# Priority offsets of the delta-rule recurrence against the projections scheduled beside it

## The chip, the cores and the metric

The kernel runs on one core of one Trainium2 chip. The metric is the device time of one execution, in microseconds; lower is better. The core has five engines that run side by side: TensorE (PE, matmuls), VectorE (DVE), ScalarE (ACT), GpSimd (POOL) and SyncE (SP, which issues most DMAs). Each engine takes its instructions in the order in which the compiled program lists them, and waits where an operand is not there yet.

## The reference

One inference step of a hybrid decoder layer over a prompt of 2048 tokens and 8 x 8 sample tokens, width 1024. RMSNorm and one input projection feed three groups of heads: A, an RWKV-7 mixer with a matrix state; B, an RG-LRU; C, an S5 state space model. Their outputs go through one output projection, then a SwiGLU block, a gated embedding and a last norm. The part that matters here is A's recurrence, which runs token by token in the reference:

```python
def step(s, inp):
    r_t, w_t, k_t, v_t, kk_t, a_t = inp
    s_kk = jnp.einsum('bhij,bhj->bhi', s, kk_t)
    s = (s * w_t[:, :, None, :]
         - s_kk[..., None] * (kk_t * a_t)[:, :, None, :]
         + v_t[..., None] * k_t[:, :, None, :])
    return s, jnp.einsum('bhij,bhj->bhi', s, r_t)
```

Its output gets a group norm per head, a bonus and a gate. The mixed rows of A, B and C, 512 + 256 + 256, are multiplied by `w_out`.

## The kernel before

The program has three stages. `phase1a` (to about 640 us) does the norm and the input projection. The sequence stage, `Phase1b.run` with `Mixers` (about 640 to 1462 us), does the recurrence, the mixers of B and C, and the output projection. `phase2` (the rest) does the SwiGLU block, the embedding and the last norm, in three blocks of 704 tokens; its first matmul is L2164.

In the sequence stage the recurrence is cut into 32 chunks of 64 tokens, in 8 units of 4 chunks. Eight heads lie in four pairs, so one product of a chunk is eight matmuls on tiles of 64 x 64 or 128 x 64 of the array, in f32. `chunk(j)` (L1607) holds the chain from state to state. In the rows its parts are: `ps_r` (L1623), the state times the chunk's keys; `R` (L1624), its copy on ScalarE; `ps_u` (L1602), the solve with the inverted triangle `Xg`; `UV` (L1605), two copies on ScalarE; `ps_s` (L1638), the update; and `SV` (L1641), two sums on VectorE that make the next state. `ps_yt` (L1650) is the chunk's output, copied to `ysb` (L1653) and stored to `yy`. Beside the chain, `front` and `prepare` make the scores of the next chunk (`ps_ak` L1533, `ps_rb` L1539, masked on VectorE) and its scaled keys (`ps_bk` L1559, `BKt` L1560), `merge` joins the inverted 32 x 32 blocks of the next unit (`ps_y` L1418, `ps_x` L1427), and `load_chunk` and `load_v` load AR, BK, UV and SV. SV and UV have two buffers each, AR three.

The other work of the stage is: the mixers of B and C (`Mixers`, among others L1099, L1189, L1263, L1264, L1284, L186); `groups_bc`, the output projection of B's and C's rows, a unit of 256 tokens at a time, each 96 matmuls of 128 x 256 with the operand `mb` (helper `mm3`, L59 to L61, in fp32r); `groups_a`, the same for A's rows with the operand `ma`, each after a group norm of its unit (`ps_cm` and `ps_var` L1819, square L1839, done in two halves, with two PSUM buffers between them); and the sample step (`sample`, `sample_a`). `groups_a` and the sample step come when `groups_bc` is done, since they reuse its memory.

What sets the order: the generators of these parts are stepped in turns (`turns`, L1958), and this gives each instruction its place in program order. A scheduler then orders each engine's instructions by simulating the program: of those that are ready it takes the one with the highest priority, which is the place in program order, moved ahead by the offset of a `high_priority` block. Four offsets stand in the recurrence: CHAIN for the links from state to state, FRONT for scores, keys, merges and loads, and OUT for the output. Mixers and projections have none. In short form, from `chunk`:

```python
            with self.tc.high_priority(offset=FRONT):
                self.front(j + 1)
                self.prepare(j + 1)
...
        with self.tc.high_priority(offset=CHAIN):
            self.solve(self.psk, X, R, UV, "ps_u")
        yield
...
        with self.tc.high_priority(offset=OUT):
            ps = self.psf("ps_yt")
```

Of the kernel before, what the change touches and what calls it, by code (L numbers as in the profile page):

```python
# [1313 lines left out]
GN_EPS = 64e-5  # L1314
NU = SEQ // 256
HALF = (slice(0, 64), slice(64, 128))
CHAIN = 300
STEP0 = 0
FRONT = 200
OUT = 200  # L1320
SMP0 = 4
SMPO = 4
MIX = 3.0
# [9 lines left out]
def halves(x):  # L1333

    return x[0:64, :, 0], x[64:128, :, 1]


class Phase1b:
# [144 lines left out]
    def chain(self):  # L1483

        yield from self.early()
        for u in range(NU):
# [4 lines left out]
            for j in range(4):  # L1491
                for _ in self.chunk(u * 4 + j, lambda h, c: self.Xg[u][h, 4 * j + c]):
                    slot += 1
                    if slot in MERGE:
                        with self.tc.high_priority(offset=FRONT):
                            next(mg, None)
                    yield
            with self.tc.high_priority(offset=FRONT):
                for _ in mg:
# [107 lines left out]
    def chunk(self, j, X):  # L1607
# [3 lines left out]
        if j < 4 * NU - 1:  # L1611
# [3 lines that stand above are left out]
        t0 = self.s2.tile([P, 4, 64], F32, name="t0")  # L1615
        R = self.s2.tile([P, 4, 64], F32, name="R")
        with self.tc.high_priority(offset=CHAIN):
            for h, x in zip(HALF, halves(SV)):
# [6 lines left out]
# [3 lines that stand above are left out]
# [3 lines left out]
        if j < 4 * NU - 1:  # L1631
            with self.tc.high_priority(offset=FRONT):
                self.load_v(SVn, j + 1)
        with self.tc.high_priority(offset=CHAIN):
            ps = self.psk("ps_s")
# [6 lines left out]

        with self.tc.high_priority(offset=OUT):
            ps = self.psf("ps_yt")
# [11 lines left out]
        if j < 4 * NU - 2:  # L1656
            with self.tc.high_priority(offset=FRONT):
                self.load_chunk(j + 2)
# [860 lines left out]
```

## Time and profile before

| | us |
|---|---|
| time, median of 3 runs | 3219.71 (3216.01 to 3224.82) |
| profiled execution, its own time | 3217.54 |
| its span, first to last instruction | 3215.8 |
| TensorE busy | 3022.9 |
| VectorE busy | 2134.8 |
| ScalarE busy | 1407.5 |
| GpSimd busy | 648.7 |

Times of instructions come from one profiled execution. A start is measured; the end of a matmul is modelled, so the distance from one start to the next says more than a matmul's own duration. An f32 matmul leaves two records, an fp32r matmul (the projections) one. The granted clock (PEclk) is the share of TensorE's full rate that the chip grants: 1.00 is 2.4 GHz, 0.50 is 1.2 GHz, and what lies between is a mean of the two.

### The profile page before, as it was taken

How to read it: one execution, taken by the hardware profiler on the slowest of the kernel's cores; microseconds unless marked ns; L12 is line 12 of the kernel's file. 1: busy time of each engine (PE TensorE's matmuls, PEld its weight loads, DVE VectorE, ACT ScalarE, POOL GpSimd, SP SyncE). 2: the span in 40 equal slices, each digit the busy share in tenths (PEclk: the TensorE clock that was granted, in tenths of full speed). 3: DMA queues.
4: the chain of work that ended last, by engine and by line, in shares of the span. 5: the costliest groups of instructions: out<-in, count | busy, mean ns of one | idle time of the engine just before them, and what ended most of it. 6: DMA issues, size and time to landing. Idle time of an engine off the chain costs nothing. (4 is left out here: it accounts for less than half of the span.)

```text
span 3215.8 us, 55092 instructions
## 1 busy us (share of the span) xinstructions
PE 3022.9 (94%) x21490; PEld 2740.7 (85%) x21490; DVE 2134.8 (66%) x3819; ACT 1407.5 (44%) x2566; POOL 648.7 (20%) x783
## 2 busy tenths in 40 slices
PE   8999999868899999996999998999999899999988
PEld 6798777656777787775999998999999899999988
DVE  4866758978764244258666676876667587667676
ACT  6555654436553333144333335533333553333354
POOL 1324434434443342230000003200000230000010
PEclk9999999958996898797999999999999999999999
DMA  6564765596654574272222223242222324222223
GB/s 198 150 186 127 212 182 158 160 234 166 175 165 134 153 211 123 70 203 94 73 75 76 72 74 103 79 133 73 73 79 70 104 72 136 79 73 79 71 78 113
DMA packets 597709, 392.92 MB, mean 122 GB/s; under 512 B 176316, under 2 KB 555720, under 8 KB 597448
## 3 DMA queue, kind: packets, MB, share of 16 engines
q1 hardware_dynamic: 589720, 371.43, 39.8%
q0 software_dynamic: 4880, 17.57, 1.5%
q8 instruction: 169, 2.77, 0.4%
q14 instruction: 92, 0.75, 0.1%
q10 hardware_dynamic: 2848, 0.40, 0.1%
HBM read 292.69 MB, written 96.62 MB: 121 GB/s over the span
## 5 line engine op out<-in xcount | busy, mean ns | idle before, releaser
L54 ACT CAST w<-raw 128x512 fp32r<-128x512 f32 (+1 forms) x438 | 258.1, 592 | 449.4 <-PE po L2141 115.2
L55 DVE TENSOR_TENSOR w<-raw,w 128x512 fp32r<-128x512 f32 (+1 forms) x438 | 303.1, 694 | 166.7 <-ACT w L54 151.9
L2151 POOL TENSOR_TENSOR acc<-acc,sq 128x704 f32<-128x704 f32 x35 | 61.7, 1762 | 1401.7 <-ACT sq L2150 1399.5
L2140 PE MATMUL po<-u,w 128*128 128x352 f32 x1056 | 341.1, 323 | 0.0
L2141 PE MATMUL po<-u,w 128*128 128x352 f32 x1056 | 340.3, 323 | 0.0
L2139 PE MATMUL po<-u,w 128*128 128x352 f32 x1056 | 324.1, 324 | 5.8 <-ACT u L54 5.8
L61 PE MATMUL ps_d<-xk,wlo 128*128 128x512 f32 (+1 forms) x800 | 286.6, 358 | 9.3 <-DVE wlo L55 9.3
L59 PE MATMUL ps_d<-xk,whi 128*128 128x512 f32 (+1 forms) x800 | 284.9, 358 | 8.1 <-ACT q__5803 L761 3.9
L54 ACT CAST w<-s 128x512 fp32r<-128x512 f32 x264 | 163.5, 621 | 290.1 <-PE po L2141 128.1
L60 PE MATMUL ps_d<-xk,whi 128*128 128x512 f32 (+1 forms) x800 | 286.0, 358 | 2.2 <-DVE xk L314 2.2
L2140 PE MATMUL pB<-xc,w 128*128 128x352 f32 x792 | 257.6, 325 | 5.6 <-DVE xc L55 5.6
L2139 PE MATMUL pB<-xc,w 128*128 128x352 f32 x792 | 256.9, 324 | 0.8 <-ACT xc L54 0.8
L2141 PE MATMUL pB<-xc,w 128*128 128x352 f32 x792 | 255.8, 323 | 0.0
L2309 DVE TENSOR_TENSOR h<-h,po 128x352 f32<-128x352 f32 x288 | 141.5, 517 | 109.5 <-PE po L2141 109.3
L55 DVE TENSOR_TENSOR w<-s,w 128x512 fp32r<-128x512 f32 x264 | 182.5, 692 | 46.7 <-ACT w L54 42.4
L2139 PEld LDWEIGHTS po<-u,w 128*128 128x128 f32 x1056 | 195.3, 188 | 6.6 <-ACT u L54 6.4
L2140 PEld LDWEIGHTS po<-u,w 128*128 128x128 f32 x1056 | 199.2, 189 | 0.9 <-DVE u L55 0.9
L2141 PEld LDWEIGHTS po<-u,w 128*128 128x128 f32 x1056 | 199.2, 189 | 0.0
L2139 PE MATMUL pA<-xc,w 128*128 128x352 f32 x528 | 173.7, 329 | 8.0 <-ACT p L2265 4.9
L61 PEld LDWEIGHTS ps_d<-xk,wlo 128*128 128x128 f32 x800 | 152.0, 190 | 31.8 <-DVE wlo L55 12.0
L2140 PE MATMUL pA<-xc,w 128*128 128x352 f32 x528 | 173.2, 328 | 5.3 <-DVE xc L55 5.3
L59 PEld LDWEIGHTS ps_d<-xk,whi 128*128 128x128 f32 x800 | 151.4, 190 | 29.7 <-ACT whi L54 5.1
(1004 smaller groups left out, 8106.2 us busy)
## 6 DMA issues: line engine op xcount, KB each, us to landing
raw<-in_w_ffn_up_dram SPq DMA_DIRECT2D x132, 512.0 KB
w<-in_w_in_dram SPq DMA_DIRECT2D x80, 512.0 KB
raw<-in_w_ffn_down_dram SPq DMA_DIRECT2D x48, 512.0 KB
sc_hT<-hp POOLq DMA_DIRECT2D x32, 512.0 KB, 4.1
raw<-in_w_ple_gate_dram SPq DMA_DIRECT2D x32, 512.0 KB
mat<-sc_mats SPq DMA_DIRECT2D x24, 512.0 KB
h<-sc_hT SPq DMA_DIRECT2D x32, 352.0 KB
raw<-in_w_ffn_down_dram SPq DMA_DIRECT2D x24, 384.0 KB
```

What stands on the lines that cost most here:

```text
L54: nc.scalar.copy(hi, src)
L55: nc.vector.tensor_sub(lo, src, hi.bitcast(F32))
L59: nc.tensor.matmul(ps, whi, xhi, start=first, stop=False)
L60: nc.tensor.matmul(ps, whi, xlo, start=False, stop=False)
L61: nc.tensor.matmul(ps, wlo, xhi, start=False, stop=last)
L2139: nc.tensor.matmul(ps, whi, xhi, start=first, stop=False, skip_group_check=more)
L2140: nc.tensor.matmul(ps, whi, xlo, start=False, stop=False, skip_group_check=more)
L2141: nc.tensor.matmul(ps, wlo, xhi, start=False, stop=last, skip_group_check=more)
L2151: eng.tensor_add(acc, acc, sq)
L2309: nc.vector.tensor_add(h[d2 * 2 + dd][:, ss], h[d2 * 2 + dd][:, ss], po[:, :SUB])
```

## The change

Three of the offsets change: CHAIN from 300 to 3000, FRONT from 200 to 2900, OUT from 200 to 2800. Nothing else does: the same instructions run on the same engines.

```diff
--- before.py
+++ after.py
@@ -1314,10 +1314,10 @@
 GN_EPS = 64e-5
 NU = SEQ // 256
 HALF = (slice(0, 64), slice(64, 128))
-CHAIN = 300
+CHAIN = 3000
 STEP0 = 0
-FRONT = 200
-OUT = 200
+FRONT = 2900
+OUT = 2800
 SMP0 = 4
 SMPO = 4
 MIX = 3.0
```

The order of the compiled program shows what that moves. It is the same up to the first chunks of the recurrence, and the same again from the last projections on. On TensorE, the update of chunk 15 (counted from 0) stands so before, `ps_s` being the update and `ps_d` a projection of B's and C's rows:

```order
L61 MATMUL ps_d<-mb,w1lo 128x256
L1638 MATMUL ps_s<-UV,BKt 64x64
L59 MATMUL ps_d<-mb,w1hi 128x256
L1638 MATMUL ps_s<-UV,BKt 64x64
L60 MATMUL ps_d<-mb,w1hi 128x256
L1638 MATMUL ps_s<-UV,BKt 64x64
L61 MATMUL ps_d<-mb,w1lo 128x256
L1638 MATMUL ps_s<-UV,BKt 64x64
L59 MATMUL ps_d<-mb,w1hi 128x256
```

And so after:

```order
L1602 MATMUL ps_u<-R,Xg_6553 64x64 x8
L1533 MATMUL ps_ak<-AR,BK 64x128 x8
L1650 MATMUL ps_yt<-AR,SV 64x64 x5
L1263 MATMUL ps_y<-U,mat 128x72
L1264 MATMUL ps_y<-H,mat 128x72
L1263 MATMUL ps_y<-U,mat 128x72
L1650 MATMUL ps_yt<-LB,UV 64x64
L1264 MATMUL ps_y<-H,mat 128x72
L1638 MATMUL ps_s<-UV,BKt 64x64 x8
L1650 MATMUL ps_yt<-LB,UV 64x64 x7
L59 MATMUL ps_d<-mb,w1hi 128x256
L60 MATMUL ps_d<-mb,w1hi 128x256
L61 MATMUL ps_d<-mb,w1lo 128x256
```

Before, every matmul of the update has a projection matmul behind it; after, the eight stand together, and the output products stand together too. The same chunk's two links on ScalarE, from the copy `R` to the copies `UV`, stand so before (the rows between are mixers, table loads and a merge):

```order
L1624 COPY R<-ps_r 128x256
L180 ACTIVATE sq<-gr 128x512
L156 CAST hi<-sq 128x512
L1265 COPY x_9708<-ps_y 128x256 x2
L188 ACT_TABLE_LOAD
L188 ACTIVATE rs<-rs 128x512
L189 ACT_TABLE_LOAD
L189 ACTIVATE rs<-rs 128x512
L1430 ACTIVATE Xg_6552<-ps_x_10755 32x16x32 x2
L1605 ACTIVATE UV<-ps_u 64x4x64 x2
```

And so after:

```order
L1624 COPY R<-ps_r 128x256
L1109 ACTIVATE gr<-gr,nsp 128x512
L1560 COPY BKt<-ps_bk 128x512
L168 ACTIVATE gq<-gl 128x512
L1265 COPY x_7850<-ps_y 128x288
L1120 ACT_TABLE_LOAD
L1120 ACTIVATE gr<-gr 128x512
L1605 ACTIVATE UV<-ps_u 64x4x64 x2
```

Ten rows have become eight; mixer instructions and a table load still stand between the links. In the second half of the stage TensorE's order before goes on to mix chunks and projections, while after it has no chunk left there. A piece from where the group norm (`ps_cm`, `ps_var`), the sample step (`ps_ry`) and the projection of A's rows meet, after the change:

```order
L61 MATMUL ps_d<-ma,w0lo 128x256
L59 MATMUL ps_d<-ma,w0hi 128x256
L60 MATMUL ps_d<-ma,w0hi 128x256
L61 MATMUL ps_d<-ma,w0lo 128x256
L1728 MATMUL ps_ry<-ax,S_11725 64x2x8 x5
L1819 MATMUL ps_cm<-hl,cm 128x512 x2
L59 MATMUL ps_d<-ma,w0hi 128x256
L60 MATMUL ps_d<-ma,w0hi 128x256
L61 MATMUL ps_d<-ma,w0lo 128x256
L59 MATMUL ps_d<-ma,w0hi 128x256
```

The recurrence's last chunk is done before this place, 1218 projection matmuls ahead of the last projection; before the change 240 were left.

## Rows read from the trace of the kernel before

**Rows 1.** page, parts 1 and 2: TensorE's busy time, share, instructions; granted clock

```profile
PE 3022.9 (94%) x21490; PEld 2740.7 (85%) x21490; DVE 2134.8 (66%) x3819; ACT 1407.5 (44%) x2566; POOL 648.7 (20%) x783
...
PEclk9999999958996898797999999999999999999999
```

**Rows 2.** windows, sequence stage: stretch, length, busy us per engine, PEclk, DMA share, GB/s

```profile
640.00:740.00 100.00, 65.45 (x785) 52.40 (x785) 75.61 (x132) 34.51 (x61) 35.56 (x42) 0.61 0.81 202
740.00:795.00 55.00, 44.13 (x707) 31.41 (x708) 46.98 (x73) 38.59 (x65) 24.41 (x28) 0.93 0.67 175
...
985.00:1060.00 75.00, 73.36 (x337) 52.62 (x337) 23.99 (x47) 12.15 (x21) 13.75 (x16) 0.55 0.29 78
...
1215.00:1385.00 170.00, 167.49 (x1572) 124.31 (x1567) 58.98 (x122) 43.56 (x102) 45.57 (x60) 0.80 0.36 102
...
sum 822.00, PE 749.91 PEld 583.67 DVE 441.66 ACT 332.83 POOL 294.49; mean PE 107.13 PEld 83.38 DVE 63.09 ACT 47.55 POOL 42.07
```

**Rows 3.** timeline, TensorE: start, us, line, out<-in; turn-taking at low clock

```profile
1011.02 0.41 PE L60 MATMUL ps_d<-mb,w1hi 128*128 128x256 f32 x1
1011.23 0.41 PE L61 MATMUL ps_d<-mb,w1lo 128*128 128x256 f32 x1
...
1013.14 0.48 PE L1650 MATMUL ps_yt<-AR,SV 128*64 128x64 f32 x2
1013.54 0.58 PE L60 MATMUL ps_d<-mb,w1hi 128*128 128x256 f32 x1
1014.06 0.48 PE L1650 MATMUL ps_yt<-AR,SV 128*64 128x64 f32 x2
```

**Rows 4.** timeline, TensorE: turn-taking at full clock

```profile
1341.35 0.32 PE L1539 MATMUL ps_rb<-AR,BK 64*64 64x64 f32 x2
1341.61 0.38 PE L61 MATMUL ps_d<-ma,w0lo 128*128 128x256 f32 x1
1341.92 0.33 PE L1539 MATMUL ps_rb<-AR,BK 64*64 64x64 f32 x2
```

**Rows 5.** timeline, TensorE: projections in a row, and the stall behind them

```profile
1460.89 0.28 PE L60 MATMUL ps_d<-ma,w0hi 128*128 128x256 f32 x1
1461.01 0.28 PE L61 MATMUL ps_d<-ma,w0lo 128*128 128x256 f32 x1
1472.33 0.96 PE L2164 MATMUL ps_st<-ah,ones 128*128 128x352 f32 x2 [11.04 <-ACT ah L54]
```

**Rows 6.** timeline, TensorE: recurrence matmuls in a row at full clock

```profile
753.04 0.69 PE L1650 MATMUL ps_yt<-AR,SV 128*64 128x64 f32 x16
753.66 0.51 PE L1650 MATMUL ps_yt<-LB,UV 64*64 64x64 f32 x10
```

**Rows 7.** timeline, TensorE: two recurrence products taking turns

```profile
937.27 0.33 PE L1638 MATMUL ps_s<-UV,BKt 128*64 128x64 f32 x2
937.53 0.33 PE L1539 MATMUL ps_rb<-AR,BK 64*64 64x64 f32 x2
937.78 0.33 PE L1638 MATMUL ps_s<-UV,BKt 128*64 128x64 f32 x2
```

**Rows 8.** VectorE: timeline of two chunk sums, then the line's first and last start

```profile
746.58 0.85 DVE L1641 TENSOR_TENSOR SV<-t,ps_s 64x256 f32<-64x256 f32 x2
...
791.08 0.42 DVE L1641 TENSOR_TENSOR SV<-t,ps_s 64x256 f32<-64x256 f32 x1
...
L1641 DVE TENSOR_TENSOR SV<-t,ps_s x64: 384/419/426, 701.7 to 1419.6; 64x256 f32<-64x256 f32 x64
```

**Rows 9.** ScalarE: timeline of group norm squares, then the line's first and last start

```profile
1410.01 0.60 ACT L1839 ACTIVATE sqb<-ps_cm 128x512 f32<-128x512 f32 x1 [0.87 <-PE ps_cm L1819]
...
1418.02 0.60 ACT L1839 ACTIVATE sqb<-ps_cm 128x512 f32<-128x512 f32 x1 [0.40 <-PE ps_cm L1819]
...
L1839 ACT ACTIVATE sqb<-ps_cm x18: 278/597/602, 1128.9 to 1440.2; 128x512 f32<-128x512 f32 x16, 128x128 f32<-128x128 f32 x2
```

## Prediction

> **What bounds the kernel now.** I read the page first, then the windows over the sequence stage, then the timeline of TensorE inside it. Matmuls fill 94% of the span [rows 1], which would say that nothing but fewer matmuls helps. The granted clock says otherwise: in its 40 slices it is near full, save between the ninth and the nineteenth, where the sequence stage lies [rows 1]. The windows cut that stage out, from 640 to 1462 us [rows 2]. TensorE counts as busy there for 749.91 of 822 us, while VectorE has 441.66, ScalarE 332.83 and GpSimd 294.49 [rows 2]. So TensorE is the engine that the stage waits for; the question is what its busy time consists of. Two windows stand out: 985 to 1060 and 1215 to 1385 have TensorE 98% busy, at a clock of 0.55 and 0.80, with VectorE at about a third of the time [rows 2].
>
> The timeline shows what runs there. One small recurrence matmul and one projection matmul take turns, and a pair takes 1014.06 - 1013.14 = 0.92 us [rows 3]. Just before, projections in a row start 0.21 us apart, at the same low clock [rows 3]. At full clock the same kind of turn-taking costs 1341.92 - 1341.35 = 0.57 us a pair [rows 4]. In a row, a projection costs 0.12 us [rows 5], and recurrence matmuls cost (753.66 - 753.04) / 8 = 0.078 us each; each f32 matmul leaves two records, so x16 is eight [rows 6]. A round trip from projection to recurrence and back therefore adds 0.57 - 0.12 - 0.078 = 0.37 us to work that is the same. Two recurrence products of different tile shape that take turns show it too: 937.78 - 937.27 = 0.51 us for two matmuls, so 0.35 us added [rows 7]. What bounds the stage is how often TensorE changes between kinds, and the low clock that goes with it.
>
> **The change part by part.** Only the order of instructions moves, so every term is a number of places in the order times a price from rows. I take all matmuls from the first of the recurrence to the last of the second projection, 4756 in both orders.
>
> A. Projection and recurrence. The order before has 541 places where one stands next to the other, the order after has 61. That is 240 round trips fewer, at 0.37 us: 89 us. I take the full-clock price and count the clock apart. At the low clock a pair adds 0.92 - 0.21 - 2 x 0.078 = 0.55 us [rows 3], so the upper bound is 132 us.
>
> B. Other changes of kind. All places where the groups projection, recurrence, mixers, group norm and sample step meet fall from 1093 to 511, which is 102 beyond A, or 51 round trips at 0.37: 19 us. Inside the recurrence, places between different products fall from 337 to 240, or 48 round trips at 0.35: 17 us. Some of these may keep the tile shape and cost nothing, so the bounds are 0 and 36; I take 36, since the row that I have shows the cost.
>
> C. The clock. Time at the lower of the two levels, 1.2 GHz, is twice the lack of granted clock: 2 x 0.45 x 75 + 2 x 0.20 x 170 = 135.5 us in the two windows [rows 2]. Work there would run twice as fast at 2.4 GHz, which gives back 68 us. A has taken part of that: of a pair of 0.92 us, all that can go is 0.92 - 0.20 = 0.72, A took 0.37, so 0.35 is left where half of the pair would be 0.46. Three quarters of 68 is 51 us. Bounds 0 (the new order is as slow elsewhere) and 68.
>
> D. Cover lost. The recurrence is a chain: product, copy on ScalarE, product, copy, product, sum on VectorE. Where it runs without projections, from 740 to 795, TensorE idles 10.9 of 55 us [rows 2] in about five chunks, so 2.0 us a chunk. The order before has eight chunks ahead of the first projection, the order after twelve, and then all 20 others with only 366 of the 1584 projection matmuls between them (44 us of work). So 24 more chunks run thinly covered: 24 x 2.0 = 48 us at most, 0 at least. I take 36, near the upper end, because on ScalarE six other rows still stand between the two links of chunk 15, a table load among them.
>
> Loads: the queue of SyncE is reordered with it, chunk loads first. They were waiting at most in the start, where the DMA share is 0.81 [rows 2]; a chunk pace twice as fast raises the share of the middle from 0.67 towards that, so I count nothing for them here and leave it to the slow rival. The tail after the last projection is untouched: its order is the same in both, and the 11.04 us stall there [rows 5] stays.
>
> Sum: 89 + 36 + 51 - 36 = 140 us. The profiled execution took 3217.54 us, 1.7 us around its span; 3217.5 - 140 = 3077.5. The median of before is 2.2 us above the profiled run, so about 3080.
>
> A second way gives the same. Chunk sums without projections beside them follow each other by (791.08 - 746.58) / 4 = 11.1 us, against (1419.6 - 701.7) / 31 = 23.2 us over the whole stage [rows 8]. At 11.1 us the 29 chunks after the one at 746.58 end near 1069. Behind them stand 1218 projection matmuls (146 us at 0.12), 72 of group norm (17 us at twice that), 288 of the sample step (22 us at 0.078), some 6 us of mixers and 215 changes of kind (40 us at 0.37 a round trip): about 231 us, so the last projection starts near 1300 plus some waits, against 1461 [rows 5]. That is 130 to 160 us.
>
> **The rivals.** First, the group norm takes over. Behind the recurrence, each half group goes through ScalarE, VectorE, TensorE and back. The closest that its squares follow each other is 1418.02 - 1410.01 = 8.0 us; over the stage it is (1440.2 - 1128.9) / 17 = 18.3 us [rows 9]. Eighteen halves at 8 us are 144 us, hidden beside the roughly 185 us that TensorE still has from the first of them on (960 projections at 0.12, and the group norm, sample step and changes of kind as above); from 10.3 us on they set the pace. At 13 us they take 234 us, so 49 us of the gain go: 3130. For it speaks that the two buffers of its PSUM pool hold one half at a time; against it that its slow stretches before are those of turn-taking. Chance 0.15.
>
> Second, more than I count: A at its upper bound, C whole and D nearly nothing, 132 + 36 + 68 - 10 = 226, so about 2990. Turn-taking lies mostly in the low-clock windows, which speaks for it. Chance 0.12.
>
> Third, slower: the chain itself becomes the bound. It decides at (1461 - 231 - 747) / 29 = 16.7 us a chunk. At 20 us the recurrence ends at 1327, the last projection at about 1560, 100 us later than now: 3320. The mechanism is the queue of ScalarE and of the loads: a link that finds six mixer instructions ahead of it, or a state buffer whose load is issued only when the output product two chunks back has read it, with the DMA engines at a share of 0.8. For it: 23.2 us is the pace now. Against it: 11.1 us was reached with VectorE 85% busy [rows 2, 8], and the slow pace lies where projections take turns. The Trainium skill, Perfetto Trace Analysis, section Optimization Strategy, advises interleaving regimes that are bound by different engines; by that rule this change goes the wrong way. The rows do not bear the rule out here: where the two are interleaved finest, both run slowest [rows 3]. Chance 0.07.
>
> Fourth, the clock stays low. A recurrence with small gaps could keep TensorE at 1.2 GHz until it ends. From 640 to 740, where it starts up with gaps, the granted clock is 0.61 [rows 2]. The 322 us from 747 to 1069 hold about 80% matmul work, 258 us at a clock of 0.93; at 0.61 that is 258 x 0.93 / 0.61 = 393, so 135 us more, and nearly all is lost: about 3215. Against it: 740 to 795 holds the same mix, without projections, at 0.93 [rows 2]. The Trainium skill, TensorE: Matmul & The Clock Gate, section Part 1: The HAM clock gate, says that the low clock is the default and that activity releases it, which fits both stretches and does not choose between them. Chance 0.04.
>
> That the change does not do what it says is ruled out by the order itself: the 32nd chunk now stands ahead of 1218 projection matmuls.
>
> **How the numbers follow.** Forecast 0.60, group norm 0.15, more 0.12, slower 0.07, clock 0.04, and 0.02 for an exchange of one loss for another at no change. A difference of 0.3% (10 us) is about what a measurement of this kernel can tell. The first three are faster: 0.60 + 0.15 + 0.12 = 0.87. The clock rival and the exchange are within 0.3%, 0.06, of which I give 0.01 to the slow side, since the clock rival's own spread reaches there: 0.05 the same, 0.08 slower. The predicted time is that of the forecast, 3080. The range takes in the group norm's 3130 with its spread, up to 3150, and reaches down to 3010, about half the way to the second rival's bound with the upper price of A; it leaves out the slow and the clock rivals and the far part of the second, together under 0.2.
>
> **What would show it.** In the profile after: TensorE's clock near full between the eleventh and the seventeenth slice; no stretch where single projections and recurrence matmuls alternate; chunk sums 10 to 13 us apart and the last near 1070 (above 16.7 us apart, the third rival); the last projection near 1320; squares of the group norm 8 to 10 us apart (above, the first rival). The prediction is wrong if the price of a change of kind does not carry over, because the recurrence's wait for ScalarE sits where the round trip sat, or if the clock stays at 0.6 while the chain runs alone.

## The result and the profile after

The changed kernel takes 3116.12 us, median of 4 runs (3115.33 to 3119.27), against 3221.94 us (3216.01 to 3224.82, 4 runs) for the kernel before: a ratio of 0.9669, 95% interval 0.9648 to 0.9689. That is 106 us faster where 140 were forecast; 3116 lies inside the range, on its slow side. The profiled execution took 3115.33 us, its span 3113.6.

The page of after, parts 1 and 2 (busy time of each engine; granted clock in 40 slices), answers [rows 1]:

```profile
PE 2881.9 (93%) x21490; PEld 2670.8 (86%) x21490; DVE 2141.3 (69%) x3819; ACT 1406.4 (45%) x2566; POOL 649.9 (21%) x783
...
PEclk9999999976898999989999999999999999999999
```

The same 21490 matmuls keep TensorE busy for 141 us less, and the busy time of VectorE, ScalarE and GpSimd changed by less than 7 us each. Where that happened the tail shows first. The timeline of TensorE in after, last projection and the stall behind it, as in [rows 5]:

```profile
1360.03 0.28 PE L61 MATMUL ps_d<-ma,w0lo 128*128 128x256 f32 x1
1371.34 0.95 PE L2164 MATMUL ps_st<-ah,ones 128*128 128x352 f32 x2 [11.04 <-ACT ah L54]
```

The last projection starts 1461.01 - 1360.03 = 101 us earlier, and the stall behind it is the same 11.04 us. All of the gain is in the sequence stage. The windows of after over that stage (start and end, length, busy us of PE, PEld, DVE, ACT and POOL, then PEclk, DMA share, GB/s), with those of [rows 2] to hold against them:

```profile
740.00:795.00 55.00, 39.09 (x561) 31.68 (x561) 37.00 (x53) 29.07 (x49) 19.20 (x20) 0.75 0.57 153
...
985.00:1060.00 75.00, 65.15 (x1056) 57.17 (x1054) 36.52 (x74) 25.06 (x52) 27.49 (x37) 0.79 0.59 156
...
1215.00:1360.00 145.00, 140.32 (x1224) 120.85 (x1223) 85.77 (x191) 57.57 (x123) 57.65 (x75) 0.98 0.68 208
sum 720.00, PE 603.26 PEld 510.02 DVE 447.37 ACT 331.32 POOL 297.46; mean PE 100.54 PEld 85.00 DVE 74.56 ACT 55.22 POOL 49.58
```

From 640 us to the last projection TensorE is busy for 603.26 of 720 us, before for 749.91 of 822 [rows 2]. So its busy time fell by 147 us (outside the stage it rose by 6, which gives the 141 of the page) and its idle time rose from 72 to 117 us, by 45: 102 us net. The prediction has the same two accounts: A + B + C = 176 us less busy, D = 36 us more idle. Both came out on the bad side, by 29 and by 9.

The recurrence and the group norm in after: the sum's and the square's row (duration min/median/max in ns, then the first and last start), as in [rows 8] and [rows 9]:

```profile
L1641 DVE TENSOR_TENSOR SV<-t,ps_s x64: 385/420/427, 696.7 to 1108.8; 64x256 f32<-64x256 f32 x64
...
L1839 ACT ACTIVATE sqb<-ps_cm x18: 278/598/602, 1175.7 to 1338.1; 128x512 f32<-128x512 f32 x16, 128x128 f32<-128x128 f32 x2
```

The last chunk sum comes at 1108.8 in place of 1419.6, a pace of (1108.8 - 696.7) / 31 = 13.3 us a chunk in place of 23.2; the forecast was 11.1 and an end near 1069. The squares follow each other by (1338.1 - 1175.7) / 17 = 9.55 us on average.

The low clock did not go where it was expected to go. Windows of before, the two longer stretches that [rows 2] does not have:

```profile
740.00:985.00 245.00, 221.83 (x2534) 169.48 (x2534) 184.22 (x315) 152.49 (x259) 114.45 (x142) 0.94 0.65 182
...
1060.00:1360.00 300.00, 292.20 (x3046) 230.23 (x3045) 106.40 (x224) 93.25 (x199) 99.64 (x129) 0.88 0.53 149
```

And the same of after:

```profile
740.00:985.00 245.00, 199.72 (x3031) 162.66 (x3029) 171.37 (x278) 155.49 (x266) 104.28 (x125) 0.86 0.61 163
...
1060.00:1360.00 300.00, 281.61 (x2817) 243.62 (x2811) 160.08 (x346) 121.11 (x257) 127.87 (x168) 0.97 0.69 207
```

Time at the lower level is twice the lack of granted clock. From 740 to 1060 it was 2 x 0.06 x 245 + 2 x 0.45 x 75 = 97 us before and is 2 x 0.14 x 245 + 2 x 0.21 x 75 = 100 us after: nothing gained. From 1060 to 1360 it falls from 72 to 18 us.

What TensorE did before the clock fell differs between the two. A window of before that has one fall in it, then a window of after that begins just behind the 2.52 us wait shown below:

```profile
1232.00:1265.00 33.00, 33.00 (x251) 23.21 (x249) 5.17 (x12) 5.04 (x11) 2.81 (x4) 0.65 0.20 58
...
758.00:774.00 16.00, 10.80 (x115) 9.27 (x112) 11.75 (x17) 9.77 (x16) 6.25 (x7) 0.50 0.44 109
```

In before, single projections and recurrence matmuls take turns there without a break, and the clock goes from 1.00 to 0.50 at 1242 us and back at 1266. Of its 16 falls between 690 and 1360 us, eight come where TensorE had gone without a wait of 0.3 us for 8 to 83 us. After has 15 falls there: ten come in the middle of a wait of TensorE, five not more than 2.1 us behind one, and these waits are 1.25 to 6.64 us long. So in these rows the low clock that is left in after comes with waits; no run takes the waits away to show that they bring it.

Where the new idle time lies, the waits of TensorE from 690 to 1110 us show. Before (what was waited for: us in total, times, longest):

```profile
PE ps_rg L1099 <- ACT gr L1100: 5.5, 3, 2.8
PE ps_d L60 <- POOL mb L1797: 4.1, 1, 4.1
PE ps_x L1427 <- DVE LB L1544: 3.8, 1, 3.8
```

After:

```profile
PE ps_rb L1539 <- DVE AR L1542: 13.9, 5, 4.3
PE ps_u L1602 <- ACT R L1624: 12.4, 5, 6.6
PE ps_r L1623 <- issue: 9.6, 6, 3.5
```

The three longest now stand before products of the recurrence: its scores (`ps_rb`), the solve (`ps_u`), and the chain's first product (`ps_r`), where "issue" means that the profile shows nothing that it waited for. The solve's wait, seen from ScalarE (timeline of after; start, us, line, out<-in):

```profile
751.64 1.99 ACT L1392 COPY xx<-X 128x1024 f32<-128x1024 f32 x1 [4.03 <-DVE X L1389]
753.53 0.68 ACT L1100 ACTIVATE gi<-ps_rg,hv 128x512 f32<-128x512 f32 x1
...
756.04 0.80 ACT L1109 ACTIVATE gr<-gr,nsp 128x512 f32<-128x512 f32 x1
756.74 0.35 ACT L1624 COPY R<-ps_r 128x256 f32<-128x256 f32 x1
```

And who waits for it on TensorE:

```profile
752.48 0.69 PE L1623 MATMUL ps_r<-SV,AR 128*64 128x64 f32 x16 [0.47 <-issue]
...
754.06 0.56 PE L1650 MATMUL ps_yt<-LB,UV 64*64 64x64 f32 x12
757.15 0.81 PE L1602 MATMUL ps_u<-R,Xg 64*64 64x64 f32 x16 [2.52 <-ACT R L1624]
```

The product that `R` copies was done near 753.2, but ScalarE takes its instructions in order: a copy of the inverses and five `ACTIVATE`s of the mixers (two shown) stand ahead of it, without a gap from 751.64 on. TensorE runs out of other work and waits 2.52 us. The scores wait in the same way for VectorE: before their longest wait ends, 4.25 us up to 1002.24, VectorE stands at mixer instructions that themselves waited 8.25 us for GpSimd (to 995.38) and 1.96 us for ScalarE (to 998.81), and the masking of `AR` comes behind them, at 1000.70.

### The profile page after: what moved, and what is told of

Its sections match the earlier page's. It is cut to its first block, busy times and chain, and to the rows that moved or that the text cites. A ratio compares the mean times of both kernels' runs of the same rounds, so it can differ in the third digit from the quotient of the medians.

```text
span 3113.6 us, 55149 instructions
## 1 busy us (share of the span) xinstructions
PE 2881.9 (93%) x21490; PEld 2670.8 (86%) x21490; DVE 2141.3 (69%) x3819; ACT 1406.4 (45%) x2566; POOL 649.9 (21%) x783
## 5 line engine op out<-in xcount | busy, mean ns | idle before, releaser
L61 PEld LDWEIGHTS ps_d<-xk,wlo 128*128 128x128 f32 x800 | 152.2, 190 | 31.1 <-DVE wlo L55 11.1
```

The lines of the kernel that those rows point to most:

```text
L61: nc.tensor.matmul(ps, wlo, xhi, start=False, stop=last)
```

## The experiments

Two sets of kernels. The first shifts the offsets between and beyond the two kernels, the second adds matmuls of the two forms behind the last gate of the kernel after, where nothing else runs, and so prices the turn-taking by itself. A change of kind is a place in TensorE's order where projection, recurrence, mixers, group norm and sample step meet, as in the prediction; its counts take each product of the mixers as a kind by itself. With the mixers as one kind the compiled orders have some 100 fewer (991 before, 405 after), and no difference to before moves by more than 12.

**Between and beyond.** One offset set each, in short form:

```diff
-CHAIN = 3000   FRONT = 2900   OUT = 2800    # after
+CHAIN = 600    FRONT = 500    OUT = 400     # d600
+CHAIN = 1700   FRONT = 1600   OUT = 1500    # d1700
+CHAIN = 300    FRONT = 2900   OUT = 2800    # nochain
+CHAIN = 0      FRONT = 0      OUT = 0       # zero
+CHAIN = 1000   FRONT = 2900   OUT = 2800    # chain1000
```

The first four were to tell the number of changes of kind (theory 1) from an early end of the recurrence (theory 2).

> Offsets CHAIN 600, FRONT 500, OUT 400: a small step of the change. TensorE's order has 363 places where projection and recurrence meet (541 before, 61 after) and 880 changes of kind in all (1093 before, 511 after); 300 projection matmuls stand behind the last chunk (240 before, 1218 after). Theory 1, changes of kind on TensorE set the time: 105.8 us for 582 changes is 0.18 us each, so 213 fewer give 39 us, about 3183. Theory 2, what counts is that the recurrence ends early so that the end of the stage is free of it: 105.8 us for 978 projections moved behind it, so 60 give 6 us, about 3215.

> Offsets 1700, 1600, 1500: a large step. 198 places projection to recurrence, 651 changes of kind in all, 720 projections behind the last chunk. Theory 1: 442 fewer changes at 0.18 us give 80 us, about 3142. Theory 2: 480 of 978 projections moved give 52 us, about 3170.

> FRONT 2900 and OUT 2800 as in the change, CHAIN left at 300: scores, keys, merges, loads and output go ahead, the links from state to state do not. 235 places projection to recurrence, 740 changes of kind in all, only 193 projections behind the last chunk, so the recurrence ends as late as before. Theory 1: 353 fewer changes at 0.18 us give 64 us, about 3158. Theory 2: nothing, about 3225.

> All three offsets 0: the recurrence stands in program order among the rest. 296 places projection to recurrence, 793 changes of kind in all, 96 projections behind the last chunk, so the recurrence ends later than before. Theory 1: 300 fewer changes at 0.18 us give 55 us, about 3167. Theory 2: 144 projections fewer behind the last chunk cost 16 us, about 3238.

> Scores, keys, loads and output at the offsets of the kernel after (2900, 2800), the links from state to state at 1000 in place of 3000. In the compiled order of the sequence stage 668 changes of kind (after 511, the links left at 300 740, before 1093) and 480 projections left behind the last chunk (1218, 193, 240). Theory 1, each change of kind has one price, 0.18 us: 3225 - 0.18 x 425 = 3148 us. Theory 3, a change removed is worth the 0.32 us that the kernel with the links at 300 showed (114 us for 353), and what is lost is cover, in proportion to the projections left behind the last chunk (79 us for the 1025 more of the kernel after): 3225 - 136 + 22 = 3111 us, about as the kernel with the links at 300 and 5 us below the kernel after. Below 3095 us if the loss of cover sets in only with the links far ahead.

| kernel | changes of kind | with those inside the recurrence | changes of tile shape | projections behind the last chunk | last chunk sum, us | TensorE busy from 640 us to the last projection, us | time, us (runs) | ratio to before, 95% |
|---|---|---|---|---|---|---|---|---|
| before | 1093 | 1430 | 1103 | 240 | 1419.6 | 749.9 | 3221.94 (4) | 1 |
| d600 | 880 | 1130 | 872 | 300 | 1372.3 | 699.8 | 3175.80 (4) | 0.9836 (0.9818 to 0.9854) |
| d1700 | 651 | 894 | 609 | 720 | 1229.2 | 624.1 | 3133.93 (4) | 0.9716 (0.9702 to 0.9731) |
| nochain | 740 | 889 | 598 | 193 | 1315.5 | 619.1 | 3110.57 (4) | 0.9646 (0.9631 to 0.9660) |
| zero | 793 | 1322 | 947 | 96 | 1395.9 | 714.5 | 3179.93 (4) | 0.9861 (0.9837 to 0.9884) |
| chain1000 | 668 | 831 | 525 | 480 | 1261.0 | 601.2 | 3104.72 (4) | 0.9648 (0.9622 to 0.9674) |
| after | 511 | 751 | 473 | 1218 | 1108.8 | 603.3 | 3116.12 (4) | 0.9669 (0.9648 to 0.9689) |

The before runs beside the first four had a median of 3224.96 us, those beside chain1000 3221.36.

Theory 2 falls. In `nochain` and `zero` the recurrence ends late, and theory 2 gave them no gain or a loss; they gained 114 and 45 us. Their sums on VectorE, nochain first:

```profile
L1641 DVE TENSOR_TENSOR SV<-t,ps_s x64: 383/420/427, 702.9 to 1315.5; 64x256 f32<-64x256 f32 x64
```

and zero:

```profile
L1641 DVE TENSOR_TENSOR SV<-t,ps_s x64: 385/424/426, 698.4 to 1395.9; 64x256 f32<-64x256 f32 x64
```

Theory 1 holds in d600, d1700 and zero, within 7, 8 and 13 us of what it gave. It misses nochain by 47 us and chain1000 by 43, both on the fast side; theory 3, formed after the first four, gave chain1000 3111 and is 6 us off. The count of the third column, chosen only after the runs, takes much of that miss away: per place between any two different products, the kernels but zero gained between 49 / 300 = 0.16 (d600 and after) and 114 / 541 = 0.21 us (nochain). That speaks for the changes inside the recurrence, as term B has it, but zero, with its 45 us for 108 places, does not fit this count.

Two further columns, likewise counted after the runs, bring zero in. A change of tile shape is a place where the part of the array that a matmul takes up (128x128, 128x64, 64x64 or 32x32) differs from the one before it. TensorE's busy time in zero, from 640 us to its last projection:

```profile
640.00:1433.50 793.50, 714.52 (x7708) 565.52 (x7708) 446.11 (x829) 332.35 (x628) 294.18 (x372) 0.85 0.61 168
```

That is 749.9 - 714.5 = 35 us less than before for 1103 - 947 = 156 places, 0.23 us each. The other five kernels save between 50 / 231 = 0.22 (d600) and 131 / 505 = 0.26 us (nochain). So in the one profiled execution of each, TensorE's busy time follows these places in all six, the clock included; what else moves the whole times is idle time and the spread of the runs, 19 us in zero. Most of the places that go change the data type as well (fp32r and f32), so the count does not tell the two apart.

The links' own offset, from 300 to 3000, is the part of the change that one can undo: nochain leaves it out and is 5.5 us below the kernel after, the intervals of the two ratios overlap. The window of nochain up to its last projection:

```profile
640.00:1353.20 713.20, 619.09 (x7708) 513.31 (x7708) 445.67 (x827) 331.11 (x628) 298.49 (x370) 0.88 0.67 186
```

TensorE is busy for 619.1 of these 713 us, so 94 are idle; after has 603.3 busy and 117 idle. The 229 changes of kind that the links' offset removes thus save 16 us of busy time, 0.07 us each, and cost 23 us of idle time. The 353 that FRONT and OUT remove without it saved 749.9 - 619.1 = 131 us, 0.37 us each, and cost 22. Both prices hold what the clock gave or took: by the windows, nochain has 71 us at the lower level from 740 to 1060 us (0.87 to 985, 0.95 behind it), where after has 100. What was dear went with FRONT and OUT; what the links' offset adds is paid back in waits and in the clock that goes with them.

**The price of a turn.** Added behind the last gate, with the kernel after unchanged ahead of them:

```diff
...
+        def dp(i):   # a projection's form, fp32r
+            ko(nc.tensor.matmul(pd[i // 24 % 2][:, :256], xs[0][0][:, 0, :128], xs[1 + i % 4][0][:, 0, :256],
+                                start=i % 24 == 0, stop=i % 24 == 23))
+        def dr(i):   # the recurrence's form, f32
+            a, c = HALF[i % 2], i // 2 % 4 * 64
+            ko(nc.tensor.matmul(pr[a, c : c + 64], h[7][a, :64], h[7][a, 64:128], start=True, stop=True))
+        for i in range(240):     # turns; blocks: 24 dp, 24 dr, ten times; fours: 4 and 4, sixty times
+            dp(i)
+            dr(i)
```

> The kernel after, with 480 matmuls added behind its last gate, whose results nobody reads: 240 of a projection's form (128 x 256, fp32r) and 240 of the recurrence's (64 x 64, f32), taking turns one by one. Nothing else is at work there, so neither buffers nor semaphores can hold them up. Theory (the price lies in the change of form itself): a pair takes about 0.57 us as in the full-clock stretch of the kernel before, 240 pairs 137 us; if the low clock comes with the turns, 0.92 us, 221 us. Rival (the turns in the kernel before were slow because each recurrence matmul waited for operands or buffers): a pair takes what its two parts take in a row, 0.12 + 0.078 = 0.20 us, and the block 48 us.

> The same 480 added matmuls, now in blocks of 24 of one form and 24 of the other, so 19 changes of form in place of 479. Theory: 240 x 0.12 + 240 x 0.078 = 48 us and 10 round trips of 0.37 us, 51 us; the difference to the turns is then 85 to 89 us, the prediction's term A for 240 round trips (170 us if the turns fall to the low clock). Rival: no difference to the turns beyond 10 us.

> The 480 added matmuls in blocks of four and four: 119 changes of form, where turns one by one have 479 and blocks of 24 have 19. With one price for each change (0.37 us a round trip): 46 + 50 x 0.37 = 65 us, the clock at 1.00. If blocks so short still bring the low clock: twice that, 110 to 130 us.

The times were 3327.68 us (turns, two runs), 3153.01 (blocks, two runs) and 3163.81 (fours, one run). The timeline of TensorE in turns, at the beginning and later:

```profile
3109.32 0.38 PE L2452 MATMUL dp<-xg 128*128 128x256 f32 x1
3109.63 0.33 PE L2457 MATMUL dr<-h 64*64 64x64 f32 x2
3109.88 0.38 PE L2452 MATMUL dp<-xg 128*128 128x256 f32 x1
...
3125.02 0.58 PE L2452 MATMUL dp<-xg 128*128 128x256 f32 x1
3125.53 0.47 PE L2457 MATMUL dr<-h 64*64 64x64 f32 x2
3125.93 0.58 PE L2452 MATMUL dp<-xg 128*128 128x256 f32 x1
```

A pair takes 3109.88 - 3109.32 = 0.56 us at first and 3125.93 - 3125.02 = 0.91 us later, the two numbers of [rows 4] and [rows 3] (0.57 and 0.92), with no wait shown from 3109.32 on. The clock fell in between, and a window of turns shows that it stays down:

```profile
3150.00:3200.00 50.00, 50.00 (x166) 31.26 (x165) 0.00 (x0) 0.00 (x0) 0.00 (x0) 0.50 0.00 1
```

The same matmuls in blocks of 24, a window:

```profile
3130.00:3152.00 22.00, 20.72 (x343) 19.64 (x341) 0.00 (x0) 0.00 (x0) 0.00 (x0) 1.00 0.01 2
```

And in fours, its window and its timeline:

```profile
3130.00:3160.00 30.00, 30.00 (x348) 24.24 (x347) 0.00 (x0) 0.00 (x0) 0.00 (x0) 1.00 0.01 2
...
3111.92 0.74 PE L2452 MATMUL dp<-xg 128*128 128x256 f32 x4
3112.59 0.45 PE L2457 MATMUL dr<-h 64*64 64x64 f32 x8
3112.97 0.74 PE L2452 MATMUL dp<-xg 128*128 128x256 f32 x4
```

The first and last starts of the two forms, in turns and then in blocks:

```profile
L2452 PE MATMUL dp<-xg x240: 383/580/580, 3108.4 to 3326.0; 128*128 128x256 f32 x120
L2457 PE MATMUL dr<-h x480: 218/312/366, 3109.1 to 3326.6; 64*64 64x64 f32 x160
...
L2452 PE MATMUL dp<-xg x240: 274/283/388, 3104.5 to 3148.9; 128*128 128x256 f32 x120
L2457 PE MATMUL dr<-h x480: 218/218/268, 3107.6 to 3150.5; 64*64 64x64 f32 x160
```

From the first start to the last the block of 480 takes 3326.6 - 3108.4 = 218 us in turns and 3150.5 - 3104.5 = 46 us in blocks, 0.19 us a pair. The 172 us between them split into 240 x (0.56 - 0.19) = 89 us for the turns at full clock and 240 x (0.91 - 0.56) = 84 us for the clock that they bring down. The first has term A's price; only the first pairs ran at full clock, so the 89 us are their price times 240. The low clock was expected as a possibility only. In fours a round trip costs (3112.97 - 3111.92) - 4 x 0.19 = 0.29 us, and the clock stays at 1.00 over the whole block. A wait of 2.42 us for VectorE stands ahead of the added matmuls in all three kernels, so it is not what tells turns from the others.

Whether the tile shape or something else makes the turn dear was asked by giving the second form the whole array:

```diff
-            a, c = HALF[i % 2], i // 2 % 4 * 64
-            ko(nc.tensor.matmul(pr[a, c : c + 64], h[7][a, :64], h[7][a, 64:128], start=True, stop=True))
+            c = i % 8 * 64
+            ko(nc.tensor.matmul(pr[:, c : c + 64], h[7][:, :128], h[7][:, 128:192], start=True, stop=True))
```

> The 480 added matmuls taking turns one by one again, but the second form is f32 on the whole array (weights 128 x 128, 64 columns) in place of 64 x 64 tiles: the data types still change at every turn, the tile shape no longer does. If it is the shape that costs: about 0.20 to 0.25 us a pair, 48 to 60 us in all, and the clock stays at 1.00. If it is the data type: as with the 64 x 64 tiles, 0.57 us a pair at full clock and 0.91 at half, 137 to 218 us.

It took 3256.03 us (one run). Timeline of TensorE in fullrows, at the beginning and later:

```profile
3101.64 0.37 PE L2452 MATMUL dp<-xg 128*128 128x256 f32 x1
3101.85 0.33 PE L2457 MATMUL dr<-h 128*128 128x64 f32 x2
3101.99 0.36 PE L2452 MATMUL dp<-xg 128*128 128x256 f32 x1
...
3140.25 0.52 PE L2457 MATMUL dr<-h 128*128 128x64 f32 x2
3140.53 0.56 PE L2452 MATMUL dp<-xg 128*128 128x256 f32 x1
3140.89 0.52 PE L2457 MATMUL dr<-h 128*128 128x64 f32 x2
```

And a window of it:

```profile
3130.00:3160.00 30.00, 30.00 (x142) 30.00 (x142) 0.00 (x0) 0.00 (x0) 0.00 (x0) 0.50 0.00 1
```

A pair takes 0.35 us at full clock, against 0.56 with the small tiles, and 0.64 against 0.91 at the low one. Neither side of the expectation is met whole. With no change of tile shape 0.21 us of the 0.37 are gone, or more, since a whole-array f32 matmul in a row was not measured and may cost more than a small one. What the other 0.35 - 0.19 = 0.16 us are, the data type or something else that changes from one matmul to the next, stays open. The clock falls to 0.50 here too, so it takes no change of shape for that. The Trainium skill, TensorEngine Tiling (Array Packing), section Key Properties, says that changing the tiling mode drains TensorE; the runs agree as far as the 0.21 us goes, and show a loss of clock besides that does not need such a change.

**A link off ScalarE.** If term D is the recurrence's links standing behind mixers on ScalarE, moving one of them should show it:

```diff
-            nc.scalar.copy(R.rearrange("p c i -> p (c i)"), ps[:, :256])
+            nc.vector.tensor_copy(R.rearrange("p c i -> p (c i)"), ps[:, :256])
```

It was made in the kernel after (rvec), in chain1000 (rvec1000) and in the kernel before (rvec300).

> The kernel after with the copy R of each chunk (the link between the state's product and the solve) on VectorE in place of ScalarE; the same numbers. Theory: the lost cover comes from links that stand behind a mixer's instructions on ScalarE; TensorE's 12.4 us of waits for R (5 waits, longest 6.6) go, and the time falls by 5 to 12 us. Rival: the link stands behind something on any engine that takes its instructions in order, VectorE is the busier one (0.73 of 690 to 985 us here), and the waits return under another name: within 5 us of the kernel after, or slower.

> The copy R on VectorE and the links at 1000: the two edits that each beat the kernel after, together. If they save different things (the wait of links behind mixers on ScalarE; cover for the end of the stage): 3105 - 21 = 3084 us. If both save the same wait: 3093 to 3100 us, no better than the better one.

> The kernel before with the copy R on VectorE and nothing else; 1098 changes of kind, 543 of them between recurrence and projections, as in the kernel before. If the copy is worth something only where the recurrence runs ahead and its links are what TensorE waits for: within 10 us of the kernel before. If a copy on VectorE saves ScalarE time whatever the order: 15 to 25 us faster than before, as it is against the kernel after.

rvec took 3095.09 us (3093.72 to 3102.5, 4 runs), ratio 0.9620 (0.9597 to 0.9643): 21 us below the kernel after, the fastest of all. rvec1000 took 3121.46, ratio 0.9689 (0.9665 to 0.9713), 17 us above chain1000; rvec300 3231.60, ratio 1.0027 (1.0003 to 1.0052). The waits of TensorE in rvec, from 690 to 1360 us, two of its rows:

```profile
PE ps_u L1602 <- DVE R L1624: 13.4, 6, 5.8
...
PE ps_rb L1539 <- DVE AR L1542: 7.9, 5, 2.1
```

The theory's own sign failed: the waits for `R` did not go, they are 13.4 us on VectorE in place of 12.4 on ScalarE. The link stands behind something on either engine, as the rival has it. The time fell all the same, by more than either expected. The window of rvec up to its last projection:

```profile
640.00:1339.70 699.70, 607.72 (x7708) 507.20 (x7708) 467.77 (x860) 321.17 (x597) 291.64 (x370) 0.88 0.68 189
```

TensorE is idle there for 92 us, in place of 117 in the kernel after, and busy for 608, in place of 603: all of the gain is idle time. The waits for `AR` shrank from 13.9 to 7.9 us and those of the first product from 9.6 to 1.8. The same edit gained nothing in the other two. The scheduler gives a new order for each edit (557 changes of kind in rvec, 666 in rvec1000), and with this one edit such orders moved by 21 us one way and by 9 and 17 us the other. So rvec is a faster kernel than both, but that it is faster because of the engine of `R` is not shown.

## Why the prediction was right, and where its sizes were off

- **What bounds the stage** held. Turns alone, with nothing else at work, cost the prices read from [rows 3 to 6] and bring the low clock with them. In the kernels between and beyond the two, TensorE's busy time follows the number of changes of tile shape, and the time does not follow the end of the recurrence.
- **Term A, 89 us**, held in its price: turns added with nothing else at work cost 0.37 us a round trip at full clock. In the whole kernel it cannot be read apart from B and C.
- **Term B, 36 us**, could not be told apart from C in size. Counted by tile shape, A and B together are 630 places, or 315 round trips: 117 us at 0.37, in place of 125.
- **Term C, 51 us, was too large.** The step that failed is that the low clock would go because its two windows go. It went behind 1060 us (72 us to 18, and the 18 us between 1360 and the old end), and came back ahead of it: 740 to 795 has 0.75 where the forecast took 0.93 to hold [rows 2]. In all it fell by some 70 us, which gives back 35, or 26 by the prediction's own three quarters: 25 of the 29 us that are missing in TensorE's busy time. In the page, slices eleven to seventeen stand at 8 or 9. That is a part of the fourth rival, the clock that stays low while the chain runs. All falls of the clock in after between 690 and 1360 us stand in or just behind a wait of TensorE, so the cover lost under D has a second price that the prediction did not give it; that is read from the rows, and no run tried it. Nor does work run twice as fast at the upper level, as term C has it: at the lower and the upper, a pair in turns takes 0.91 and 0.56 us, projections in a row start 0.21 and 0.12 us apart [rows 3, 5].
- **Term D, 36 us, was too small:** 45 us of new idle time, close to the upper bound of 48 (10.9 us over five chunks is 2.2 a chunk, not 2.0, which makes the bound 52). The pace of 11.1 us was 13.3 over all. It was read from the four quickest chunks of the start; the two ahead of them had taken 19.4 and 25.4 us. It also runs from a chunk's first sum to another's second, which starts 1.1 us behind its first. The slower pace is the whole of the miss in the second way of the sum: the recurrence ended 1108.8 - 1069 = 40 us late, and the part behind it took 1360 - 1109 = 251 us, as forecast (231 and waits, 1320 - 1069 = 251). The mechanism is the one the slow rival names, links that find mixers ahead of them on engines that take work in order, seen on ScalarE at 751 to 757 us, and for the scores on VectorE at 995 to 1002 us, where the prediction had looked at ScalarE alone; it stopped at 13.3 us a chunk, short of the 16.7 from which it loses.
- **Group norm** did not take over: squares 9.55 us apart, under the 10.3 that decide, and TensorE busy for 140.32 of the last 145 us.
- **Tail:** the same stall of 11.04 us, as forecast.
- **Luck.** That 3116 lies in the range is in part luck: its slow side, from 3080 to 3150, was made for the group norm's 3130, and what came out there instead were the clock and the lost cover.
- **Interleaving.** The rule of the Trainium skill, Perfetto Trace Analysis, section Optimization Strategy, on interleaving regimes of different engines has two sides here. Finest interleaving on TensorE was the loss that the change removed; but the links' offset, which pulls the two apart altogether, saved 16 us of busy time and lost 23 as idle time (nochain against after). nochain and chain1000, where runs of both alternate, keep most of both.

## What to carry to other kernels

Before one asks whether TensorE is busy, one should look at what it alternates between: two forms of small matmul that take turns one by one can cost nearly five times what they cost in runs (218 us against 46), and a profile that says 98% busy hides it. Priority between two streams is worth setting so that each comes in runs of a few matmuls; beyond that, pulling the streams further apart gave back in waits here what it saved in changes. A pace read from the few quickest rounds is a best case, to be used with the full lost cover beside it, and waits that the new order brings can cost clock as well.

## What the runs showed of the hardware

Turn-taking of two matmul forms one by one brings the granted clock from 1.00 to 0.50 and keeps it there for more than 200 us, to the end of the block, though the records show TensorE busy for 50.00 of 50.00 us (turns; 30.00 of 30.00 in fullrows, without a change of tile shape); in runs of four, the same matmuls keep 1.00. The Trainium skill, TensorE: Matmul & The Clock Gate, section Part 1: The HAM clock gate, has activity release the low clock; in these rows TensorE counts as busy throughout and the clock is low, so of the two columns only PEclk tells it. The clock is thus a second price of the turns, here 84 us for 240 of them beside the 89 us that they cost at full clock.
